# Down projection: seven places instead of three for the raw operands of the block products, and other load and product times in the scheduler

## The chip, the core and the metric

The kernel runs on one core of one Trainium2 chip, as one launch. The metric is the device time of the launch in microseconds (us), the median of several executions; less is better. All data are float32; matmul operands are the 32-bit "fp32r" type, and each product of two float32 operands is made of three matmuls (below).

## What is computed

One inference step of one encoder layer, for 1024 prompt tokens and 32 sample tokens: a normalised input projection, three recurrent mixers (GLA, HGRN2, mLSTM), an output projection, and a feed-forward block with a causal convolution over time. The change lies in the last part, cut here to what matters:

```
def conv_ffn(xn, buf, w_up, conv_w, conv_b, w_down):
    up = xn @ w_up                                   # 1024 -> 2 * 2816
    up, buf = causal_dwconv(up, buf, conv_w, conv_b) # 3 taps
    gate, val = jnp.split(up, 2, axis=-1)
    return (jax.nn.gelu(gate, approximate=True) * val) @ w_down, buf   # 2816 -> 1024
    ...
    x = x + rms_norm(h, g_ffn_post[l])
```

## The kernel before

**Three matmuls per product.** An operand is split into a high half (a cast to fp32r on ScalarE, line 95) and a low half (raw minus high on VectorE, line 98). `mm3` (lines 89 to 91) then adds high x high, high x low and low x high into one PSUM bank. On TensorE every product therefore shows as L89, L90 and L91.

**The stages.** The program runs through the input projection with the mixers and the output projection (tiles `pf`, `pv`, `zp`, `fxt` and the 64-row matmuls of line 773), then the up projection (`pux`, `puw`, `puy`, `puz`; 22 blocks `f` of 128 features, each with its convolution and gelu), then the down projection in `down_all`. The down projection has two parts.

1. The **first part** (tiles `pd`, called the pd stage here) takes 288 token columns (units 0, 8 and 4) the plain way: for each of the 22 `f` it loads `hr` (three pieces of `h_d`, line 1360) and 512 KB of weights `wd` (line 1363), splits both, and does 8 x 3 matmuls of 128x288. Beside that it forms sums of weight blocks (`sums`, lines 1231 to 1234) from pairs of `wd` tiles and stores them to `t_d` (line 1236). `hr` has two buffers, `wd` four (tag `wide`).
2. The **second part** (called the seven products here) takes the other six units of 128 tokens by a Strassen-Winograd scheme of seven block products p1 to p7, run in the order p1, p2, p6, p5, p3, p7, p4. Each is `seven(p, ps, first)`: for `k` = 0 to 10 it loads one raw tile `r` (named `rp` in the profile) in two transfers, 256 KB of weights or weight sums (line 1409) and 192 KB of activations or activation sums (line 1408). From `r` come four halves: `wdp` (weights, high and low in one tile, seven buffers) and `hhp`, `hlp` (activations, two buffers each for odd and for even `k`). Three token units x 3 matmuls of 128x512 follow, into the banks `pdx` (p1, p6, p7, p4), `pdy` (p2) or `pdw` (p5, p3). Between products the banks are copied out or added to `cu` and `cl`; `finish_half` and `finish_end` (lines 1324, 1326, 211, 212, 1335) normalise and add the residual, and line 1336 stores the result.

**Where raw tiles lie.** In before, `r` has tag `y0` with three buffers of the pool `ph` (the pool of the up projection's tiles, which is still open). A fourth load can be issued only when all four halves of the first of the three have been made: when the second subtraction of that tile (`hlp` or `wdp`, line 98) is through. The same pool holds the tags `y1` (one buffer), `bw` (two) and `st` (one), which the up projection fills and nothing uses later.

**What sets the order.** Nothing runs in the order in which it is written. `order` builds a graph of all instructions and `play` places them engine by engine, on its own table of costs; the engine then runs its list in that order, whatever is ready. In that table a load or store issued on SP (SyncE) queues behind the one before, takes its transfer time, and counts as landed 650 ns after that (`stop = queue + 650`); `PRODUCT` gives the time of a matmul by its width. Every cast, subtraction and matmul that depends on a load is placed by these figures, in the whole program. If a load comes later than its place in the list, the engine stands there, and what follows in its list waits too.

Of the kernel before, what the change touches and what calls it, by code (L numbers as in the profile page):

```python
# [9 lines left out]
F32 = mybir.dt.float32  # L10
# [21 lines left out]
NCOL = 2 * HW  # L32
# [9 lines left out]
def fcol(u):  # L42

    return 128 * u if u < 4 else SMP if u == 8 else GAP_P + 2 + 128 * (u - 4)
# [35 lines left out]
def body(ctx: ExitStack, tc: tile.TileContext, a: dict):  # L80
# [1073 lines left out]
    def weight_halves(name, src):  # L1154
        t = praw[1].tile([128, 2, 512], F32R, tag="op", name=name, bufs=7)
        split(t[:, 0], t[:, 1], src, dve)
        return t[:, 0], t[:, 1]
# [71 lines left out]
    def sums(k, ws):  # L1229
        (b11, b12), (b21, b22) = ((t[:, :512], t[:, 512:]) for t in ws)  # L1230
        dve.tensor_tensor(b11, b12, b11, op=ALU.subtract)
        dve.tensor_tensor(b12, b22, b12, op=ALU.subtract)
        dve.tensor_tensor(b22, b22, b11, op=ALU.subtract)
        dve.tensor_tensor(b21, b21, b22, op=ALU.subtract)
        for i in range(2):
            sp.dma_start(t_d[k, i], ws[i])
# [68 lines left out]
    def down_all(ph, p6, gp):  # L1305
        xres = {}

        def wide(name):
            return p6.tile([128, 1024], F32, tag="wide", name=name, bufs=4)

        def residual(u):
            n = 128 if u < 8 else DEC
            x = p6.tile([128, 1024], F32, tag="xres", name=f"fr{u}", bufs=3)
            sp.dma_start(x[:n], x2_d[128 * u:128 * u + n, :])
            xres[u] = x
# [27 lines left out]
        def h_halves(name, w, r, pool_, tag):  # L1343
            hh, hl = (pool_.tile([128, 384], F32R, tag=f"{tag}{x}", name=f"h{x}{name}", bufs=2) for x in "hl")
            split(hh[:, :w], hl[:, :w], r, dve)
            return hh, hl


        off, w = {}, 0
        for u in FIRST:  # L1350
            off[u] = w
# [2 lines left out]
        banks = [p.tile([128, 512], F32, tag=t, name=f"pd0_{i}", bufs=b) for i, (p, t, b) in enumerate(where)]  # L1354
        pair = []
        for f in range(NF):
            r = ph.tile([128, 288], F32, tag="hr", name=f"hr{f}", bufs=2)
            for u in FIRST:
                n = 128 if u < 8 else DEC
                sp.dma_start(r[:, off[u]:off[u] + n], h_d[f, :, fcol(u):fcol(u) + n])  # L1360
            hh, hl = h_halves(f"0_{f}", w, r, ph, "h")
            wr = praw[0].tile([128, 1024], F32, tag="raw", name=f"wd0_{f}r", bufs=2) if f < 2 else                 wide(f"wd0_{f}r")
            sp.dma_start(wr, a["w_dn"][f])
            wd = [weight_halves(f"wd0_{f}{hf}", wr[:, 512 * hf:512 * hf + 512]) for hf in range(2)]
            pair.append(wr)
            if f % 2:
                if f // 2 >= len(EARLY):
                    sums(f // 2, pair)
                pair = []
            if f == NF - 6:  # L1370
                sp.dma_start(gp, a["grows"][1:2, :].broadcast_to([128, 1024]))
                for u in FIRST:
                    residual(u)
            for d in range(8):
                c = slice(128 * (d % 4), 128 * (d % 4) + 128)
                mm3(banks[d][:, :w], [t[:, c] for t in wd[d // 4]], (hh[:, :w], hl[:, :w]), f == 0, f == NF - 1)
# [27 lines left out]
        def seven(p, ps, first):  # L1404
            ops = []
            for k in range(NP):
                r = ph.tile([128, NCOL], F32, tag="y0", name=f"r{p}_{k}", bufs=3)
                sp.dma_start(r[:, :384], ASRC[p](k))
                sp.dma_start(r[:, 384:896], BSRC[p](k))
                hh, hl = h_halves(f"{p}_{k}", 384, r[:, :384], *((ph, "h") if k % 2 else (p6, "g")))  # L1410
                wd = weight_halves(f"wd{p}_{k}", r[:, 384:896])
                ops.append((k, hh, hl, wd))
                if k == NP - 2:
                    continue
                for i in range(3):
                    c = slice(128 * i, 128 * i + 128)
                    for (j, hh, hl, wd) in ops:
                        mm3(ps[i], (hh[:, c], hl[:, c]), wd, first and j == 0, j == NP - 1, skip_group_check=True)
                ops = []
                if k % 3 == 0 and todo:  # L1420
                    todo.pop(0)()
# [173 lines left out]
AHEAD = {"mx": 10000., "psm": 10000., "pdx0": 1400., "pdx1": 700., "pdw0": 1400., "pdw1": 700., "pt": 130000.}  # L1595
ENGINES = ("PE", "DVE", "Activation", "Pool", "SP")
WINDOW = 3413.3
PRODUCT = {512: 232., 384: 175.5, 288: 133.5, 282: 131.5, 274: 126.5, 256: 118.}
PACKET = ((4, 9), (32, 9), (128, 13), (256, 18), (512, 27), (1024, 46), (1536, 65), (2048, 84), (4096, 159), (8192, 330), (1 << 16, 2640))
TABLES = {"Ln": 5, "Gelu_apprx_tanh": 11, "Exp": 0, "Tanh": 0, "Square": 0}  # L1600

# [94 lines left out]
def _product(i):  # L1696
# [9 lines left out]
    if mode == (128, 128) or (mode == (128, 32) and not f32) or mode == (32, 128):  # L1706
        g = PRODUCT.get(n, n / 2.4 + 12) if not f32 else max(n * 2 / 2.4 + 2.5, 60) if tr else 2 * max(n * 2 / 2.4 + 8, 112)
        return g, True, (128, 128) if mode == (128, 32) else mode, cells, (r, sums)
# [160 lines left out]
def play(g, tail, change, slack=None):  # L1869
# [6 lines left out]
    rows, held, seen, known, count = {}, [], [-1] * len(g.pred), dict.fromkeys(ENGINES, -1), 0  # L1876
    port, queue = {"DVE": 0., "Pool": 0.}, 0.
# [24 lines left out]
    while True:  # L1902
        t, e = min(((free[e] if ready[e] else max(free[e], at[wait[e][0][2]]), k) for k, e in enumerate(ENGINES) if ready[e] or wait[e]),
                   default=(None, None))
        if e is None:
            break
        e = ENGINES[e]
        while wait[e] and wait[e][0][0] <= t + 1e-6:
            heapq.heappush(ready[e], heapq.heappop(wait[e])[1:])
        if not ready[e]:  # L1910
            heapq.heappush(ready[e], heapq.heappop(wait[e])[1:])
        if e == "PE" and len(ready[e]) > 1:
            c = min(heapq.nsmallest(12, ready[e]), key=lambda x: x[0] + (change if mm[x[1]][2] != mode else 0))
            ready[e].remove(c)
            heapq.heapify(ready[e])
        else:
            c = heapq.heappop(ready[e])
        n = c[1]
        t = max(t, at[n])
        d, own, lock = cost[n]  # L1920
        sync = max([known[e]] + [seen[q] for q in g.pred[n] if eng[q] != "PE" or e != "PE"])
        if e == "PE" and any(k in rows and rows[k][0] != mm[n][4][0] and rows[k][1] > sync for k in mm[n][4][1]):
            held.append(c)
            continue
        if e == "SP" and queue - t - 1400 > BACKLOG:
            heapq.heappush(ready[e], c)
            free[e] = queue - 1400 - BACKLOG + 5
            continue
        if e == "Pool" and lock and port["DVE"] > t:
            heapq.heappush(ready[e], c)  # L1930
            free[e] = port["DVE"] + 5
            continue
        if e == "SP":
            free[e] = t + own
            queue = max(t + 1400, queue) + d
            stop = queue + 650
        elif e == "PE":
            d, wide, m, cl, (row, sums) = mm[n]
            if mode not in (None, m):
                t = max(t, max(cells) + (93 if mode == (128, 128) else 45))  # L1940
            mode, t = m, max([t] + [cells[c] for c in cl])
            if wide:
                free[e] = clock.run(t, d)
                cells = [free[e]] * 16
                stop = free[e] + 166
            else:
                f = clock.factor(t)
                for c in cl:
                    cells[c] = t + d * f
                clock.add(t, 14)  # L1950
                free[e] = t + 14 * f
                stop = t + d * f + 168
        else:
            if e == "DVE" and lock:
                t = max(t, port["Pool"])
                port["DVE"] = t + d
            if e == "Pool" and lock == 1:
                port["Pool"] = t + d
            if g.table[n] not in (None, table):
                table = g.table[n]  # L1960
                t += 1283
            free[e], stop = t + own, t + d
        if e == "PE":
            rows.update((k, (row, count)) for k in sums)
            seen[n], count = count, count + 1
            if sync > known[e]:
                while held:
                    heapq.heappush(ready[e], held.pop())
        else:
            seen[n] = sync  # L1970
        known[e] = sync
        start[n], end[n] = t, stop
        seq[e].append(n)
        release(n)
# [143 lines left out]
```

## Time and profile before

| | |
|---|---|
| median of 3 runs | 1357.84 us (1354.48 to 1359.75) |
| the profiled execution | 1356.24 us |
| its span in the trace | 1354.4 us |
| TensorE (PE) busy | 1303.9 us, 96% of the span |
| VectorE (DVE) busy | 1039.2 us, 77% |
| ScalarE (ACT) busy | 710.6 us, 52% |
| GpSimd (POOL) busy | 181.9 us, 13% |
| moved by DMA | 285.24 MB, mean 211 GB/s |

The profiled execution lies 1.84 us above its span (what lies outside the first and last instruction) and 1.6 us below the median. PE busy is the union of modelled, pipelined matmuls: a lone matmul is shown with 0.39 us while back to back ones start more closely, so that a short wait of PE can vanish in it. In the profile, "idle before, releaser" after a group says how long its engine stood idle just before it and what ended that. SPq rows are transfers being issued on SP's queue; "DMA rp<-t_d" is the flight of such a transfer until it landed.

### The profile page before, as it was taken

To read this page: it belongs to the slowest core of one execution; us is meant where nothing else is said; L and a number is where in the kernel's file an instruction comes from. 1 tells how busy PE (TensorE), PEld (TensorE's weight loads), DVE (VectorE), ACT (ScalarE), POOL (GpSimd) and SP (SyncE) were. 2 spreads that over 40 slices of the span, in tenths; PEclk is the share of its full clock that TensorE was granted. 3 is DMA by queue.
4 is the path that set the end of the run, shared out by engine and by line. 5 is a ranking of instruction groups with operands and counts; after the bars stand their busy time and mean duration, and the time that the engine had idled before them with its cause. 6 is when DMAs were issued, how large, how long until landed. Compare 5 with 4: busy or idle time off the path is not lost.

```text
span 1354.4 us, 30370 instructions
## 1 busy us (share of the span) xinstructions
PE 1303.9 (96%) x11977; PEld 1207.9 (89%) x11977; DVE 1039.2 (77%) x1884; ACT 710.6 (52%) x1400; POOL 181.9 (13%) x331
## 2 busy tenths in 40 slices
PE   6999999999999999999899999999999999998997
PEld 5999999998898887678899999999999999886775
DVE  6795549757889468878899988888888877755576
ACT  5654556545576554436754544545545454555554
POOL 2010100100102112222012211111111110000011
PEclk9999999999999999999999999999999999999998
DMA  9899869976898964635156623323223189786675
GB/s 327 260 330 332 266 243 333 301 260 203 287 305 288 331 231 121 202 95 171 69 199 230 215 97 109 102 87 119 80 87 119 71 275 290 261 265 192 218 248 205
DMA packets 148422, 285.24 MB, mean 211 GB/s; under 512 B 30039, under 2 KB 84471, under 8 KB 148279
## 3 DMA queue, kind: packets, MB, share of 16 engines
q1 hardware_dynamic: 148279, 283.30, 62.2%
q8 instruction: 94, 1.54, 0.5%
q14 instruction: 49, 0.40, 0.1%
HBM read 201.90 MB, written 81.34 MB: 209 GB/s over the span
## 4 chain that ended last, share of the span: by engine, by line
PE 69%; DMA 14%; DVE 9%; ACT 4%; issue 3%; SPq 1%; POOL 0%; DVEq 0%; ACTq 0%; POOLq 0%
PE pux L91 4%; PE pux L89 4%; PE pux L90 4%; PE pv L89 4%; PE pv L91 4%; PE pv L90 4%; DMA rp<-t_d 4%; PE pf L89 3%; PE pf L91 3%; PE pf L90 3%; PE puw L90 3%; PE puw L91 3%; PE puw L89 3%; DMA rp<-in_w_dn 2%; PE zp L89 2%
## 5 line engine op out<-in xcount | busy, mean ns | idle before, releaser
L1250 DVE SCALAR_TENSOR_TENSOR y<-uu,fconv_sb,y 128x1060 f32<-128x1060 f32 x88 | 115.8, 1320 | 7.9 <-ACT y L1248 7.4
L98 DVE TENSOR_TENSOR wdp<-rp,wdp 128x512 fp32r<-128x512 f32 x77 | 53.2, 691 | 56.2 <-ACT wdp L95 55.9
L95 ACT CAST wdp<-rp 128x512 fp32r<-128x512 f32 x77 | 47.7, 620 | 70.4 <-DMA rp<-t_d 39.0
L1248 ACT ACTIVATE y<-uu,fconv_sb 128x1060 f32<-128x1060 f32 x44 | 56.1, 1278 | 25.9 <-POOL uu L1245 21.5
L1196 ACT COPY c<-pux 128x274 f32<-128x274 f32 (+1 forms) x132 | 46.3, 381 | 33.9 <-PE pux L91 30.1
L926 POOL TENSOR_TENSOR hrs<-hss,mhalf 128x5 f32<-128x5 f32 (+3 forms) x27 | 35.8, 1330 | 175.3 <-DVE hss L925 172.6
L89 PE MATMUL pv<-wt_0h,xh 128*128 128x256 f32 (+2 forms) x195 | 53.8, 297 | 2.6 <-DVE xl L309 1.3
L91 PE MATMUL pv<-wt_0h,xl 128*128 128x256 f32 (+2 forms) x195 | 51.7, 288 | 0.0
L90 PE MATMUL pv<-wt_0l,xh 128*128 128x256 f32 (+2 forms) x195 | 51.5, 287 | 0.0
L89 PE MATMUL pdx<-wdp,hhp 128*128 128x512 f32 x132 | 44.8, 404 | 6.7 <-ACT hhp L95 4.6
L89 PE MATMUL pv<-wt_1h,xh 128*128 128x256 f32 (+2 forms) x195 | 49.1, 288 | 0.0
L91 PE MATMUL pv<-wt_1h,xl 128*128 128x256 f32 (+2 forms) x195 | 48.6, 288 | 0.0
L1245 POOL COPY uu<-fcache_sb 128x2 f32<-128x2 f32 x44 | 23.4, 531 | 186.1 <-DVE uu L1201 186.1
L90 PE MATMUL pv<-wt_1l,xh 128*128 128x256 f32 (+2 forms) x195 | 48.3, 288 | 0.0
L98 DVE TENSOR_TENSOR hlp<-rp,hhp 128x384 fp32r<-128x384 f32 x77 | 41.8, 552 | 5.4 <-ACT hhp L95 2.9
L90 PE MATMUL pdx<-wdp,hhp 128*128 128x512 f32 x132 | 43.9, 395 | 0.0
L91 PE MATMUL pdx<-wdp,hlp 128*128 128x512 f32 x132 | 42.9, 395 | 0.1
L95 ACT CAST hhp<-rp 128x384 fp32r<-128x384 f32 x77 | 38.4, 511 | 5.8 <-PE pdx L90 3.1
L89 PEld LDWEIGHTS pv<-wt_0h,xh 128*128 128x128 f32 (+1 forms) x195 | 35.2, 189 | 4.6 <-DVE xl L309 1.6
L211 POOL TENSOR_SCALAR gss<-gss 128x1 f32<-128x1 f32 (+1 forms) x9 | 7.4, 817 | 233.7 <-ACT gjk L1324 158.2
L89 PEld LDWEIGHTS pdx<-wdp,hhp 128*128 128x128 f32 x132 | 24.8, 191 | 13.9 <-ACT hhp L95 6.7
L808 DVE COPY_PREDICATED P<-masks_sb,sc 128x352 f32<-128x352 int32 (+1 forms) x44 | 29.8, 678 | 8.8 <-PE sc L773 8.3
(1781 smaller groups left out, 5144.4 us busy)
## 6 DMA issues: line engine op xcount, KB each, us to landing
h_d<-y SPq DMA_DIRECT2D x22, 530.0 KB, 5.1
rp<-t_d SPq DMA_DIRECT2D x44, 256.0 KB, 3.8
wt_0r<-in_w_tok SPq DMA_DIRECT2D x21, 512.0 KB, 5.9
wt_1r<-in_w_tok SPq DMA_DIRECT2D x21, 512.0 KB, 5.0
rp<-in_w_dn SPq DMA_DIRECT2D x33, 256.0 KB, 3.7
rp<-s_d SPq DMA_DIRECT2D x44, 192.0 KB, 3.9
wt_0l<-lt_d SPq DMA_DIRECT2D x14, 512.0 KB, 4.7
wt_1l<-lt_d SPq DMA_DIRECT2D x14, 512.0 KB, 5.8
```

Source lines behind the costliest of these rows:

```text
L89: pe.matmul(ps, lh[0], rh[0], start=first, stop=False, **kw)
L90: pe.matmul(ps, lh[0], rh[1], start=False, stop=False, **kw)
L91: return pe.matmul(ps, lh[1], rh[0], start=False, stop=last, **kw)
L95: act.copy(hi, src)
L98: (eng or pool).tensor_tensor(lo, src, hi.bitcast(F32), op=ALU.subtract)
L211: pool.tensor_scalar(out, ss, other, EPS, op0=ALU.add, op1=ALU.add)
L808: dve.copy_predicated(dst, mk_.broadcast_to([n, 11, *mk_.shape[2:]]), src)
L926: pool.tensor_tensor(rs[:n, h0:h0 + nh], ss[:n, h0:h0 + nh], mhalf[:n, :nh], op=ALU.pow)
L1196: act.copy(t, ps)
L1245: pool.tensor_copy(u[:, GAP_S:GAP_S + 2], fcache[:, j, :])
L1248: act.activation(y, u, AF.Identity, scale=fconv[:, j, 2:3], bias=fconv[:, j, 3:4])
L1250: dve.scalar_tensor_tensor(y, uu[i][:, s:s + NCOL], fconv[:, j, s:s + 1], y, op0=ALU.mult, op1=ALU.add)
```

## The change

- The raw tiles of the seven products go round seven places: `y0`, `bw`, `y0`, `y1`, `y0`, `bw`, `st`. All seven are 128x896 or larger already, so no memory is added. The fourth load no longer waits for the first tile, the eighth does.
- In the pd stage, `hr` uses the two `bw` buffers for every other pair of `f`, which makes four places of two.
- In the cost table a transfer counts as landed 1250 ns after its transfer time instead of 650 ns, and the six matmul times move by 0.5 to 4.5 ns.

```
+        places = [("y0", 3), ("bw", 2), ("y0", 3), ("y1", 1), ("y0", 3), ("bw", 2), ("st", 1)]
+        def raw(name):
+            t, b = places[count[0] % 7]
+            count[0] += 1
+            return ph.tile([128, 896], F32, tag=t, name=name, bufs=b)
...
-            r = ph.tile([128, 288], F32, tag="hr", name=f"hr{f}", bufs=2)
+            r = ph.tile([128, 288], F32, tag="hr", name=f"hr{f}", bufs=2) if f % 4 < 2 else \
+                ph.tile([128, 288], F32, tag="bw", name=f"hr{f}", bufs=2)
...
-                r = ph.tile([128, NCOL], F32, tag="y0", name=f"r{p}_{k}", bufs=3)
+                r = raw(f"r{p}_{k}")
...
-PRODUCT = {512: 232., 384: 175.5, 288: 133.5, 282: 131.5, 274: 126.5, 256: 118.}
+PRODUCT = {512: 227.5, 384: 175., 288: 132.5, 282: 131., 274: 127., 256: 119.5}
...
-            stop = queue + 650
+            stop = queue + 1250
```

Since the cost table serves the whole program, the lists of all engines change from the first stage on, with the same work in them. Two places matter for the prediction.

ScalarE, at the start of p6 (raw tiles `rp_k` with the weight halves `wdp_k` and the activation halves `hhp_k`; the last number only names a buffer). Before:

```order
L95 CAST wdp_2_15961<-rp_2_15954 128x512
L95 CAST wdp_3_15980<-rp_3_15973 128x512
L95 CAST hhp_2_15957<-rp_2_15954 128x384
L95 CAST hhp_3_15976<-rp_3_15973 128x384
L1324 ACTIVATE gjk_16560,gss_16559<-cu_15693 128x512
L95 CAST wdp_4_15999<-rp_4_15992 128x512
L95 CAST hhp_4_15995<-rp_4_15992 128x384
```

The same place of the changed kernel:

```order
L95 CAST wdp_3_15980<-rp_3_15973 128x512
L95 CAST hhp_0_15919<-rp_0_15916 128x384
L95 CAST wdp_4_15999<-rp_4_15992 128x512
L95 CAST hhp_3_15976<-rp_3_15973 128x384
L95 CAST wdp_5_16018<-rp_5_16011 128x512
L95 CAST hhp_2_15957<-rp_2_15954 128x384
L95 CAST hhp_4_15995<-rp_4_15992 128x384
```

Before, the activation cast of tile 2 stands behind the weight cast of tile 3, the newest of the tiles on its way; the two casts of a tile are neighbours. In the changed kernel the weight casts run up to three tiles ahead of the activation casts.

SP, in the last third of the pd stage (`hr` and `wd` are that stage's loads, `t_d<-wd` its stores, `rp_k` the first loads of p1). Before:

```order
L1363 DMA wd_15r<-in_w_dn 128x1024
L1409 DMA rp_2_15476<-in_w_dn 128x512
L1360 DMA hr_14964<-h_d 128x128 x2
L1360 DMA hr_14964<-h_d 128x32
L1408 DMA rp_2_15476<-h_d 128x384
L1236 DMA t_d<-wd_12r 128x1024
L1360 DMA hr_15004<-h_d 128x128 x2
L1360 DMA hr_15004<-h_d 128x32
L1236 DMA t_d<-wd_13r 128x1024
```

The same place of the changed kernel:

```order
L1372 DMA wd_15r<-in_w_dn 128x1024
L1417 DMA rp_2_15476<-h_d 128x384
L1418 DMA rp_4_15537<-in_w_dn 128x512
L1369 DMA hr_15050<-h_d 128x128 x2
L1369 DMA hr_15050<-h_d 128x32
L1417 DMA rp_4_15537<-h_d 128x384
L1236 DMA t_d<-wd_12r 128x1024
L1369 DMA hr_15090<-h_d 128x128 x2
L1369 DMA hr_15090<-h_d 128x32
L1418 DMA rp_6_15575<-in_w_dn 128x512
L1417 DMA rp_6_15575<-h_d 128x384
L1236 DMA t_d<-wd_13r 128x1024
```

Ahead of the last `wd` load (`wd_21r`) before has issued three raw tiles of p1 (0, 1 and 2), the changed kernel six (0, 3, 2, 4, 6 and 1); three more tiles of 448 KB have moved from the seven products into the pd stage.

More of the change, by code (lines that the diff above doesn't have):

```diff
@@ L1346, in h_halves @@
             return hh, hl
+        places = [("y0", 3), ("bw", 2), ("y0", 3), ("y1", 1), ("y0", 3), ("bw", 2), ("st", 1)]
+        count = [0]
+        def raw(name):
+            t, b = places[count[0] % 7]
+            count[0] += 1
+            return ph.tile([128, 896], F32, tag=t, name=name, bufs=b)
         off, w = {}, 0
```

## Prediction

> **What bounds the kernel now.** First the page's table of engines: TensorE (PE) is busy nearly throughout, so a gain must come from stretches in which it waits or is clocked down. The stages one by one show where; columns are stretch, length, then busy time with number of instructions for PE, PEld, DVE, ACT, POOL, then granted clock, DMA share and GB/s.
>
> ```profile
> 0.00:620.00 620.00, 594.37 (x6960) 537.28 (x6961) 449.70 (x982) 330.45 (x688) 82.12 (x126) 0.99 0.78 260
> 620.00:1098.50 478.50, 473.06 (x3774) 468.55 (x3773) 414.84 (x607) 247.13 (x447) 84.31 (x182) 1.00 0.36 127
> 1098.50:1171.70 73.20, 70.94 (x528) 69.56 (x527) 59.73 (x101) 38.81 (x74) 2.10 (x5) 1.00 0.92 302
> 1171.70:1197.30 25.60, 25.60 (x128) 21.06 (x127) 19.25 (x35) 14.76 (x35) 4.60 (x6) 1.00 0.79 252
> 1197.30:1221.00 23.70, 23.17 (x101) 18.23 (x99) 12.39 (x22) 12.93 (x25) 0.00 (x0) 1.00 0.74 234
> 1221.00:1245.40 24.40, 21.83 (x92) 17.13 (x93) 15.50 (x28) 12.20 (x24) 0.00 (x0) 1.00 0.62 199
> 1245.40:1295.40 50.00, 47.53 (x207) 38.37 (x206) 25.89 (x45) 25.92 (x50) 0.00 (x0) 1.00 0.66 211
> 1295.40:1346.80 51.40, 47.42 (x199) 37.70 (x197) 37.97 (x65) 27.70 (x60) 6.62 (x9) 0.97 0.70 232
> 1346.80:1354.40 7.60, 0.00 (x0) 0.00 (x0) 3.91 (x6) 0.69 (x2) 2.12 (x4) 0.74 0.55 208
> ```
>
> The rows are: mixers and projections, up projection, pd stage, then p1, p2, p6, p5 with p3, p7 with p4, and the tail. The up projection leaves PE 5.4 us idle in 478. The seven products leave more than their busy column says, because a lone matmul is shown longer than its turn. The turn is read where nothing is waited for, from the starts of two groups of three:
>
> ```profile
> 1201.36 0.84 PE L89 MATMUL pdy<-wdp,hhp 128*128 128x512 f32 x3
> ...
> 1202.04 0.84 PE L90 MATMUL pdy<-wdp,hhp 128*128 128x512 f32 x3
> ...
> 1173.75 0.44 PE ptxw L1389 x4
> ```
>
> 0.68 us for three is 0.227 us each. The products hold 7 x 11 x 9 = 693 such matmuls, 157.1 us, and 24 transposes in six groups of four at 0.44 us (last row, from the chain of waits), 2.6 us. With a few last `pd` matmuls that is 160 us, in a stage of 175.1 us (1171.7 to 1346.8): **15 us of slack**, mostly from p6 on. What ends it, in the waits:
>
> ```profile
> ACT wdp L95 <- DMA rp<-t_d: 39.0, 33, 2.1
> ACT wdp L95 <- DMA rp<-in_w_dn: 28.6, 22, 2.9
> ...
> PE pdx L89 <- ACT hhp L95: 4.6, 4, 2.0
> PE pdx L89 <- DVE cl L1454: 2.1, 1, 2.1
> PE pdw L89 <- ACT hhp L95: 1.7, 1, 1.7
> ...
> PE pdw L89 <- ACT cl L1445: 0.8, 1, 0.8
> ...
> PE pdy L89 <- ACT hhp L95: 0.2, 1, 0.2
> ```
>
> ScalarE stands 67.6 us before loads and passes some on to PE as missing `hhp`. One turn of one place shows how (p6, tile 2, then tile 5 in the same place):
>
> ```profile
> 1219.07 0.32 SPq L1409 DMA_DIRECT2D rp<-t_d  x1
> ...
> 1222.22 0.62 ACT L95 CAST wdp<-rp 128x512 fp32r<-128x512 f32 x1 [1.29 <-DMA rp<-t_d]
> ...
> 1224.64 0.62 ACT L95 CAST wdp<-rp 128x512 fp32r<-128x512 f32 x1 [1.80 <-DMA rp<-t_d]
> 1225.17 0.92 ACT L95 CAST hhp<-rp 128x384 fp32r<-128x384 f32 x2
> ...
> 1225.73 0.97 PE L89 MATMUL pdx<-wdp,hhp 128*128 128x512 f32 x3 [2.02 <-ACT hhp L95]
> 1225.90 1.02 DVE L98 TENSOR_TENSOR hlp<-rp,hhp 128x384 fp32r<-128x384 f32 x2
> ...
> 1226.48 0.32 SPq L1409 DMA_DIRECT2D rp<-t_d  x1
> ```
>
> Issue 1219.07, cast 3.15 us later; then ScalarE, whose list has the weight cast of tile 3 next, waits until 1224.64, and tile 2's activations, long there, are cast at 1225.17. Only the subtraction behind that frees the place: 7.41 us for three tiles, where PE needs 3 x 9 x 0.227 = 6.13. So two things bind: three places, and a list made for loads landing earlier than they do.
>
> **The change, part by part.** *(a) Seven places.* With PE at full pace a place comes round every 7 x 2.04 = 14.3 us. It is held from issue to landing and for its casts (all instructions on `rp`: least, median and longest ns):
>
> ```profile
> L95 ACT CAST hhp<-rp x77: 494/511/526, 1110.3 to 1341.1; 128x384 fp32r<-128x384 f32 x77
> L98 DVE TENSOR_TENSOR hlp<-rp,hhp x77: 535/552/559, 1114.6 to 1341.8; 128x384 fp32r<-128x384 f32 x77
> L95 ACT CAST wdp<-rp x77: 605/621/625, 1165.1 to 1337.7; 128x512 fp32r<-128x512 f32 x77
> L98 DVE TENSOR_TENSOR wdp<-rp,wdp x77: 673/692/694, 1165.8 to 1338.3; 128x512 fp32r<-128x512 f32 x77
> L1409 SPq DMA_DIRECT2D rp<-t_d x44: 319/320/663, 1213.2 to 1334.5; - x44
> L1408 SPq DMA_DIRECT2D rp<-s_d x44: 422/432/1464, 1213.7 to 1310.0; - x44
> ...
> DMA to landing us min/median/max: 2.9/4.0/5.6
> ```
>
> Taking the slowest landing, 5.6, plus the 4.3 us from first cast (1222.22) to the end of both subtractions (1226.48) in the bad turn above, it is 9.9 us, 4.4 us to spare. Bandwidth allows it: 448 KB per 2.04 us is 225 GB/s, which p2 (234) already moved. SP issues two transfers per tile, 0.75 us of 2.04; the four halves cost ScalarE 1.13 and VectorE 1.24 us of 2.04. Result stores stand in SP's list among these loads, and SP stands at each until VectorE has its `fr`; what queues behind has those 4.4 us in hand. So PE becomes the bound. What is late next are the bank turns: the 0.8 us before p3 (`cl` copies) stays; of the 2.1 before p4 about 1.2 stays (the add into `cl` takes 0.68 and has other VectorE work ahead of it). With 1.5 for the start of p1 and for ScalarE's turn order, 3.5 us remain. Gain: 15 - 3.5 = **11.5 us**. Ends: the five PE rows above sum to 9.4 us, and if only these go, less the 3.5, it is 6; and 14 if only 1 us stays.
>
> *(b) The pd stage.* Four `hr` places remove ScalarE's waits for `hr` and so at most PE's 2.2 us. Against that, three raw tiles of 448 KB each now share this stage's transfers, which already move 302 GB/s at a DMA share of 0.92:
>
> ```profile
> ACT hh L95 <- DMA hr<-h_d: 9.0, 8, 2.7
> ...
> PE pd L89 <- ACT hh L95: 2.2, 5, 0.7
> ...
> 1139.91 5.46 DMA wd_17r<-in_w_dn
> ```
>
> 1.38 MB at 302 GB/s is 4.6 us, and a `wd` flight of 5.5 us is on the chain that ends last here. In SP's list the added loads stand ahead of `wd_16r` to `wd_21r`, so these, their sums and their stores queue behind. Ends: -2.2 and +4.6; the middle, **+1 us**, since neither row outweighs the other.
>
> *(c) Landing at 1250 ns and matmul times.* In the seven products this is in (a): activation casts no longer stand behind the newest load. Elsewhere the lists change with the same work. The trace has no row for that; the nearest is PE's idle time, 25.6 us in the first 620 and 5.4 in the up projection. I take **0**, with ends of 7 us either way: about a quarter of those 31 us.
>
> *The tail* after the last matmul (7.6 us) has the same instructions: 0.
>
> **Sum**: -11.5 + 1 + 0 = -10.5 us, 1345.7 for the profiled execution's 1356.24. That execution lies 1.6 below the median, so for the median 1357.84 - 10.5 = **1347.3 us**, 0.8% faster. What a measurement here can tell from no change is about 0.5%, 6.8 us.
>
> **Rivals.** *Crowded pd stage.* All 4.6 us of (b) are lost and (a) gives its low 6: 1357.84 - 6 + 4.6 = 1356.4. For it speaks the share of 0.92; against, that the same bytes leave the products, where there is room.
>
> *Loads were never the bound.* If a turn took the least landing (2.9 us), 0.75 for its two issues and 1.7 for its chain of halves (0.62, 0.51 and 0.55), it would be 5.35, under 6.13, and three places would do; only the two bank turns would shift. Then perhaps 2 us go: 1356. Against it: the measured turn of 7.41 and the median landing of 4.0. The Trainium skill ("DMA: Bandwidth & Descriptors", Anatomy of one DMA — SWDGE (gpsimd) path) has a rule that would say this: about 2.0 us fixed plus bytes at 436 GB/s, so by estimate 2.6 us for 256 KB, stated for the GpSimd path. The trace disagrees for SP's loads: 4.0 us.
>
> *Slower: the first 620 us lose their clock.* A gap of about 2 us halves TensorE's pace after it, as before p4:
>
> ```profile
> 1321.36 0.68 DVE L1454 TENSOR_TENSOR cl<-cl,pdx 128x512 f32<-128x512 f32 x1
> ...
> 1322.18 0.47 PE L89 MATMUL pdx<-wdp,hhp 128*128 128x512 f32 x1 [2.12 <-DVE cl L1454]
> ...
> 1323.62 0.63 PE L90 MATMUL pdx<-wdp,hhp 128*128 128x512 f32 x1
> ...
> 1324.05 0.63 PE L89 MATMUL pdx<-wdp,hhp 128*128 128x512 f32 x1
> ```
>
> The starts are 0.43 apart instead of 0.227; the granted clock of 0.97 over these 51.4 us is a loss of 1.5 us, so 2.1 + 1.5 = 3.6 us per gap. The new lists of the mixer stage, where PE hangs on casts and 64-row work, could hold more such gaps. From five more on (18 us) the forecast's gain is turned into a loss of more than the bound: 1347.3 + 18 = 1365.3. For it: every list there changes; against: with 600 ns more the table's landing is nearer to what the loads take, so waits should get fewer. (The Trainium skill, "TensorE: Matmul & The Clock Gate", Part 1, names an idle window of about 3.4 us for the halving; here 2.1 us of idle sufficed.)
>
> *The early stages gain too*, by (c)'s full 7 us: 1340.3.
>
> **How the numbers follow.** Forecast 0.62, crowded 0.11, never the bound 0.08, slower 0.08, early gain 0.11. Range: from the early gain with (a) at its 14, 1357.84 - 14 + 1 - 7 = 1338, to the two rivals at 1356 with 2 us of spread, 1358; what lies outside is the slower case and an edge of the others. Faster by over 0.5% (below 1351): 0.60 of the forecast's 0.62, and the early gain: 0.71. Within 0.5%: both middle rivals and the forecast's 0.02: 0.21. Slower: 0.08.
>
> **What would show it.** Right: in the seven products PE's rows add to some 163 to 165 us; ScalarE's waits for `rp` fall from 67.6 to under 20; `PE <- ACT hhp` all but goes; the granted clock of p7 and p4 is 1.00. The pd stage shows its cost as longer waits of `wd` casts for loads. Wrong: the products still take over 170 us, or the stretch up to the first `pd` matmul differs from 1098.5 by over 7 us.

## The result and the profile after

The changed kernel takes 1348.71 us, the median of five executions (1344.93 to 1350.66), against 1357.84 for before (1352.63 to 1360.38): a ratio of 0.994, 95% interval 0.9911 to 0.9969, or 9.1 us less where 10.5 were forecast. Its profiled execution is the fastest of the five: 1344.93 us, span 1343.1, against 1356.24 and 1354.4.

Before's span, cut at three places that both kernels have: the first matmul of the up projection (`pux`), the first of p2 (`pdy`), the end of the last matmul. Columns are those of the stages in the prediction.

```profile
0.00:633.90 633.90, 608.26 (x7021) 548.67 (x7022) 461.91 (x992) 342.43 (x709) 85.27 (x128) 0.99 0.77 258
633.90:1197.30 563.40, 555.70 (x4365) 547.77 (x4364) 481.61 (x732) 288.71 (x532) 87.86 (x191) 1.00 0.45 155
1197.30:1346.70 149.40, 139.92 (x595) 111.43 (x593) 91.64 (x157) 78.74 (x159) 6.52 (x9) 0.99 0.68 220
1346.70:1354.40 7.70, 0.03 (x1) 0.00 (x0) 4.01 (x7) 0.69 (x2) 2.23 (x4) 0.74 0.54 205
```

The changed kernel at the same places:

```profile
0.00:636.90 636.90, 609.41 (x7020) 547.48 (x7021) 461.59 (x992) 343.14 (x709) 88.44 (x128) 0.99 0.77 257
636.90:1198.90 562.00, 554.60 (x4361) 546.70 (x4361) 479.73 (x732) 290.77 (x536) 88.44 (x191) 1.00 0.46 157
1198.90:1335.40 136.50, 136.00 (x599) 111.97 (x597) 93.06 (x155) 78.70 (x155) 7.28 (x11) 1.00 0.72 234
1335.40:1343.10 7.70, 0.00 (x0) 0.00 (x0) 4.11 (x7) 0.69 (x2) 1.50 (x3) 0.80 0.54 205
```

| stretch | before | after | difference |
|---|---|---|---|
| start to first `pux` (mixers, projections) | 633.9 | 636.9 | +3.0 |
| first `pux` to first `pdy` (up projection, pd stage, p1) | 563.4 | 562.0 | -1.4 |
| first `pdy` to the last `pdx` (p2 to p4) | 149.4 | 136.5 | -12.9 |
| tail | 7.7 | 7.7 | 0 |

PE's pause in p2 to p4 falls from 9.5 us (149.40 - 139.92) to 0.5, and its clock there rises from 0.99 to 1.00. The waits of the changed kernel in p2 to p4 show who waits for whom now:

```profile
ACT hhp L95 <- PE pdx L90: 13.1, 15, 2.2
...
DVE hlp L98 <- PE pdw L91: 10.6, 13, 1.6
...
DVE hlp L98 <- DMA rp<-s_d: 2.2, 3, 0.7
ACT wdp L95 <- DMA rp<-in_w_dn: 2.1, 2, 1.3
...
ACT hhp L95 <- DMA rp<-s_d: 1.5, 2, 0.7
ACT wdp L95 <- DMA rp<-t_d: 1.5, 2, 1.0
```

The casts of weights wait 3.6 us for loads (2.1 + 1.5), against 58.2 in the same stretch of before (its two rows stand under e3 below); ScalarE and VectorE now wait for PE to give up `hhp` and `hlp`. The same can be seen at the turn from p2 to p6, and something that was not forecast:

```profile
1219.00 0.32 SPq L1418 DMA_DIRECT2D rp<-t_d  x1
...
1219.29 0.39 PE L89 MATMUL pdx<-wdp,hhp 128*128 128x512 f32 x1
...
1220.40 0.52 ACT L95 CAST hhp<-rp 128x384 fp32r<-128x384 f32 x1 [1.42 <-PE pdy L90]
...
1223.80 0.52 ACT L95 CAST hhp<-rp 128x384 fp32r<-128x384 f32 x1 [1.64 <-PE pdy L90]
...
1224.50 0.84 PE L91 MATMUL pdy<-wdp,hlp 128*128 128x512 f32 x3
```

p6 (`pdx`) begins at 1219.29 while p2 (`pdy`) goes on until after 1224.50. The list that PE has now laps one product over the next, and so the bank turns have cover.

### The profile page after: what moved, and what is told of

Its sections match the earlier page's. It is cut to its first block, busy times and chain, and to the rows that moved or that the text cites. A ratio compares the mean times of both kernels' runs of the same rounds, so it can differ in the third digit from the quotient of the medians.

```text
span 1343.1 us, 30434 instructions
## 1 busy us (share of the span) xinstructions
PE 1300.0 (97%) x11977; PEld 1206.1 (90%) x11977; DVE 1038.5 (77%) x1884; ACT 713.3 (53%) x1400; POOL 185.7 (14%) x331
## 4 chain that ended last, share of the span: by engine, by line
PE 81%; DMA 7%; DVE 7%; ACT 3%; issue 2%; SPq 0%; POOL 0%; DVEq 0%; ACTq 0%; POOLq 0%
PE pux L89 5%; PE pux L90 5%; PE pux L91 5%; PE pv L89 4%; PE pv L90 4%; PE pv L91 4%; PE pf L89 3%; PE puw L91 3%; PE puw L89 3%; PE puw L90 3%; PE pf L91 3%; PE pf L90 3%; PE zp L89 2%; PE pdx L89 2%; PE pdx L90 2%; PE pdx L91 2%
## 5 line engine op out<-in xcount | busy, mean ns | idle before, releaser
L98 DVE TENSOR_TENSOR hlp<-rp,hhp 128x384 fp32r<-128x384 f32 x77 | 42.6, 556 | 37.6 <-ACT hhp L95 12.2
L926 POOL TENSOR_TENSOR hrs<-hss,mhalf 128x5 f32<-128x5 f32 (+3 forms) x27 | 40.7, 1532 | 172.3 <-DVE hss L925 172.1
L91 PEld LDWEIGHTS pv<-wt_0h,xl 128*128 128x128 f32 (+1 forms) x195 | 34.2, 189 | 0.8 <-issue 0.4
```

The source lines that it names most:

```text
L91: return pe.matmul(ps, lh[1], rh[0], start=False, stop=last, **kw)
L98: (eng or pool).tensor_tensor(lo, src, hi.bitcast(F32), op=ALU.subtract)
L926: pool.tensor_tensor(rs[:n, h0:h0 + nh], ss[:n, h0:h0 + nh], mhalf[:n, :nh], op=ALU.pow)
```

## The experiments

Each kernel is timed beside before on the same chip: e1 to e4 on one chip (before's median there 1353.44 us), a2, e5, e10 and e11 on a second (1354.76), e6, e8, e12 and e13 on a third (1354.57). The ratio to that median has its 95% interval behind it; the other columns come from each kernel's one profile. "Load waits" are ScalarE's and VectorE's waits for `rp` in p2 to p4. "Idle" is the stretch up to the first `pux` less PE's busy time in it. "Clock loss" is the same stretch cut into 31 equal windows, (1 - granted clock) x length summed.

| kernel | ratio | first `pux` | idle | clock loss | `pux` to `pdy` | p2 to p4 | load waits |
|---|---|---|---|---|---|---|---|
| before | 1 | 633.9 | 25.6 | 4.9 | 563.4 | 149.4 | 59.9 |
| after | 0.994 [0.9911, 0.9969] | 636.9 | 27.5 | 5.1 | 562.0 | 136.5 | 7.8 |
| a2_after | 0.9955 [0.9935, 0.9974] | 637.8 | 24.1 | 10.5 | 566.2 | 136.3 | 9.5 |
| e1_places | 0.9902 [0.9877, 0.9927] | 628.9 | 22.4 | 3.2 | 563.1 | 136.8 | 16.2 |
| e2_costs | 0.9962 [0.9945, 0.998] | 637.4 | 26.4 | 6.8 | 563.3 | 141.3 | 53.3 |
| e3_late_rp | 0.994 [0.9917, 0.9963] | 634.1 | 24.7 | 6.5 | 561.7 | 140.3 | 54.3 |
| e4_places_late_rp | 0.9897 [0.9873, 0.9922] | 634.8 | 25.3 | 6.8 | 563.1 | 136.3 | 15.3 |
| e8_four | 0.9865 [0.9826, 0.9904] | 629.4 | 24.3 | 3.5 | 560.3 | 136.2 | 35.2 |
| e5_hr_two | 0.9966 [0.9944, 0.9988] | 636.0 | 26.6 | 6.8 | 565.9 | 136.2 | 7.9 |
| e6_p1_three | 0.9879 [0.9842, 0.9917] | 630.2 | 24.2 | 3.3 | 561.3 | 136.4 | 12.1 |
| e10_old_product | 0.9895 [0.9865, 0.9925] | 631.9 | 24.0 | 5.1 | 563.9 | 136.1 | 10.7 |
| e11_old_landing | 0.9956 [0.9935, 0.9977] | 636.9 | 24.9 | 8.4 | 564.6 | 136.4 | 12.0 |
| e12_half | 0.9865 [0.9833, 0.9897] | 628.1 | 23.2 | 3.2 | 561.7 | 136.0 | 10.1 |
| e13_mirror | 0.9843 [0.981, 0.9875] | 621.2 | 21.0 | 0.0 | 565.3 | 137.3 | 12.2 |

Eleven of the fourteen kernels share three sets of lists up to the first `pux`: the order of instructions on every engine is the same in the traces of before, e1, e3 and e4, in those of after, a2, e2 and e5, and in those of e6, e8 and e10 (but for up to 35 places in 7020 of PE's, all 64-row matmuls whose recorded starts change places). The first `pux` spans 628.9 to 634.8 in the first set, 636.0 to 637.8 in the second and 629.4 to 631.9 in the third. So one list gives up to 5.9 us of spread between profiles, and a single profile can't tell two lists apart by less.

The theory was that the ring of three places bound the products (R in the expectations); the first rival, that it was the order of the lists, made for loads landing too early (O).

### What freed the products

**e1_places**: the places alone, with the old cost table.

```
-                r = ph.tile([128, NCOL], F32, tag="y0", name=f"r{p}_{k}", bufs=3)
+                r = raw(f"r{p}_{k}")
```

(with `raw`, its table of seven and the four places of `hr`)

> Seven places and the four hr places, with the cost table of before (landing 650 ns, old matmul times). The lists of all engines up to the middle of the up projection are those of before. Theory R (the ring of three places binds): p2 to p4, from the first pdy matmul to the end of the last pdx matmul, falls from 149.5 us to 136 to 140; pd stage with p1 is 99 to 101 us against 98.8; the time is 8 to 12 us under before. Rival O (the list made for early landing binds, places matter little): p2 to p4 stays above 144 us and the time is within 5 us of before.

p2 to p4 take 136.8 us: the places alone take away 12.6 of the 12.9. The time is 13.4 us under before (1353.44 - 1340.08), more than R's 8 to 12. The kernel as a whole looks better than with the whole change (0.9902; the whole change 0.994 and, repeated, 0.9955); its interval is clear of that of the repeat, not of that of the first measurement.

**e2_costs**: the cost table alone, three places.

```
-PRODUCT = {512: 232., 384: 175.5, 288: 133.5, 282: 131.5, 274: 126.5, 256: 118.}
+PRODUCT = {512: 227.5, 384: 175., 288: 132.5, 282: 131., 274: 127., 256: 119.5}
...
-            stop = queue + 650
+            stop = queue + 1250
```

> Three places as before, with the cost table of the changed kernel (landing 1250 ns, new matmul times) for the whole program; the mixers and projections have the lists of the changed kernel. Theory R: p2 to p4 stays between 145 and 150 us, since a place still takes over 7 us for three tiles; the time is 0 to 4 us under before. Rival O: p2 to p4 falls below 143 us. Rival H (the new lists of the early stages give the gain): the first pd matmul comes over 4 us earlier than in before, and the time is 6 us or more under before with p2 to p4 unchanged.

**e3_late_rp**: before, with 1250 ns for the loads into `rp` alone.

```
+        self.late.append(name.startswith("rp"))
...
-            stop = queue + 650
+            stop = queue + (1250 if g.late[n] else 650)
```

> Before, with the landing of 1250 ns for the raw tiles of the seven products alone (three places, all else 650 ns). The lists up to the end of the pd stage are those of before but for a few rows. Theory R: p2 to p4 146 to 150 us, the time within 4 us of before. Rival O: p2 to p4 below 143 us, the time 6 us or more under before.

Here R missed. With three places p2 to p4 still come down to 141.3 and 140.3 us, by 8 to 9. The waits of e3 in p2 to p4 show that this isn't mainly because loads are waited for less:

```profile
ACT wdp L95 <- DMA rp<-t_d: 36.6, 32, 2.6
ACT wdp L95 <- DMA rp<-in_w_dn: 15.9, 12, 2.8
...
PE pdx L89 <- ACT hhp L95: 1.3, 2, 1.1
```

Before, in the same stretch, the first two were:

```profile
ACT wdp L95 <- DMA rp<-t_d: 39.0, 33, 2.1
ACT wdp L95 <- DMA rp<-in_w_dn: 19.2, 15, 2.8
```

ScalarE waits 52.5 us instead of 58.2, yet PE waits 1.3 for these `hhp` where it waited 4.6. ScalarE's list at that place of e3 tells why:

```profile
1224.33 0.62 ACT L95 CAST wdp<-rp 128x512 fp32r<-128x512 f32 x1 [1.30 <-DMA rp<-t_d]
1225.13 0.52 ACT L95 CAST hhp<-rp 128x384 fp32r<-128x384 f32 x1 [0.17 <-DMA rp<-s_d]
1226.69 0.62 ACT L95 CAST wdp<-rp 128x512 fp32r<-128x512 f32 x1 [1.05 <-DMA rp<-t_d]
1227.27 0.51 ACT L95 CAST hhp<-rp 128x384 fp32r<-128x384 f32 x1
```

Here each tile's activations follow its own weights. In before's list the activations of tile 2 stood behind the wait for tile 3, and went out late by that much.

**e4_places_late_rp**: both of these remedies, matmul times as before.

```
 (the edit of e1_places and that of e3_late_rp)
```

> Seven places and four hr places, 1250 ns for the raw tiles of the seven products alone, the rest of the cost table as in before: the lists of the mixers and projections are those of before. Theory R: p2 to p4 135 to 138 us and the time 9 to 12 us under before, at most 2 us better than seven places alone. Rival O: over 4 us better than seven places alone. Rival H: since the early lists are those of before, over 4 us worse than the changed kernel.

136.3 us. So the two remedies are for the same waits: 12.6 by places, 9.1 by the order (149.4 - 140.3), 13.1 by both. The time is 13.1 us under before, above R's 9 to 12; it is no better than with places alone (0.9897 and 0.9902), and H, which had it 4 us worse than the changed kernel, falls.

**e8_four**: four places, all transfers at 1250 ns, old matmul times.

```
-        places = [("y0", 3), ("bw", 2), ("y0", 3), ("y1", 1), ("y0", 3), ("bw", 2), ("st", 1)]
+        places = [("y0", 3), ("y0", 3), ("y0", 3), ("y1", 1)]
```

> Four places (three y0 and y1) for the raw tiles, with hr on bw, landing 1250 ns and the old matmul times; the lists up to the pd stage are those of the changed kernel with the old matmul times. A place then turns in 8.2 us of PE time for four tiles, against landing plus casts of some 6.5 us. Theory R+ (a ring of three is short by under one tile once the list is right): p2 to p4 within 1.5 us of the 136 us of seven places. Rival: it falls halfway, 138 to 140 us, because the slow landings of over 5 us need more places.

136.2 us: with lists made for 1250 ns, one place more than three is enough. Four places with the old table were not run. In its p2 to p4 ScalarE still waits 34.8 us for loads, and PE keeps going:

```profile
DVE wdp L98 <- ACT wdp L95: 30.2, 31, 2.3
ACT wdp L95 <- DMA rp<-t_d: 25.4, 23, 2.5
...
ACT wdp L95 <- DMA rp<-in_w_dn: 9.4, 9, 1.9
```

One of its six executions took 3197.4 us; it is left out of the ratio, and its cause is unknown.

### The pd stage

**e5_hr_two**: the changed kernel with `hr` on two buffers again.

```
-            r = ph.tile([128, 288], F32, tag="hr", name=f"hr{f}", bufs=2) if f % 4 < 2 else \
-                ph.tile([128, 288], F32, tag="bw", name=f"hr{f}", bufs=2)
+            r = ph.tile([128, 288], F32, tag="hr", name=f"hr{f}", bufs=2)
```

> The changed kernel with hr on its two buffers alone, so that bw belongs to the raw tiles from the first. My term for the pd stage said at most 2.2 us for the four hr places: the time is 0 to 2.5 us over the changed kernel, and the stretch from the first pux to the first pdy matmul 0 to 2.5 us longer. Rival: the hr places cost by holding back tile 1 of p1, which then lands too late; then it is 0 to 3 us under.

**e6_p1_three**: three places for p1, so that p1's early loads can't crowd the pd stage, seven from p2 on; old matmul times.

```
-            t, b = places[count[0] % 7]
+            t, b = places[count[0] % 7] if count[0] > 10 else ("y0", 3)
```

> Seven places from p2 on, but three for p1, with landing 1250 ns and the old matmul times: the first loads of p1 no longer move into the pd stage beyond before's three. If the crowding of the pd stage costs (my term: 4.6 us at most), the stretch from the first pux to the first pdy matmul is 1 to 4 us shorter than with seven places throughout (563.9), and the time 0.986 to 0.989 of before. If not, p1 itself misses its places: the stretch is 0 to 2 us longer and the time 0.989 to 0.992.

By their times both are inconclusive. e5 (0.9966) lies in the interval of its yardstick a2_after (0.9955), e6 (0.9879) in that of e10_old_product (0.9895), though e6's time and its stretch of 561.3 both fall where the crowding was to put them. From the first `pux` to the first `pdy` the changed kernel itself took 562.0 and 566.2 us in its two profiles; differences of 1 or 2 us can't be told within that. What can be told is where the waits went. In the changed kernel, from the first `pd` to the first `pdy`:

```profile
ACT wd L95 <- DMA wd_16r<-in_w_dn: 3.9, 1, 3.9
ACT wd L95 <- DMA wd_21r<-in_w_dn: 3.7, 1, 3.7
ACT wd L95 <- DMA wd_20r<-in_w_dn: 2.9, 1, 2.9
...
PE pd L89 <- ACT hh L95: 1.9, 2, 1.4
...
ACT wd L95 <- DMA hr<-h_d: 1.0, 1, 1.0
```

ScalarE's waits for `wd_16r` to `wd_21r` rose from 10.2 us to 17.2 and those for `hr` fell from 9.0 to 1.0; PE's wait for `hh` went from 2.2 to 1.9.

All fourteen profiles together tell more. Take PE's idle time from the first `pd` to the first `pdy` and add the clock loss there (in windows of 5 us). In the five kernels that give p1 fewer than seven places it is 2.3 (before), 0.9 (e2), 1.9 (e3), 0.8 (e8) and 1.5 us (e6). In the nine that give it seven it is 2.0 (e12), 2.4 (after), 4.2 (e4), 4.6 (e13), 4.7 (e10), 4.8 (e11), 5.2 (e1), 6.0 (a2) and 6.2 (e5). In seven of these nine, and in none of the five, 1.7 us of it is lowered clock. The means are 1.5 and 4.5: seven places in p1 go with some 3 us more lost in this stage. With one profile per kernel this is a strong tendency, not a proof. (e1 took 102.6 us from the first `pd` to the first `pdy`, where 99 to 101 were expected.) The changed kernel's own profile, at 2.4, is one of the luckiest of its group.

### The early stages

**a2_after**: the changed kernel again, as the yardstick for e5, e10 and e11.

> The changed kernel once more, as the yardstick for this group, since seven places alone came out at 0.990 of before and the changed kernel at 0.994. Theory H- (the new lists of the early stages cost some 5 us): 0.993 to 0.996 again. Rival N (the difference was the draw of clock gaps and the chip): 0.989 to 0.992.

**e10_old_product**: the changed kernel with the old matmul times.

```
-PRODUCT = {512: 227.5, 384: 175., 288: 132.5, 282: 131., 274: 127., 256: 119.5}
+PRODUCT = {512: 232., 384: 175.5, 288: 133.5, 282: 131.5, 274: 126.5, 256: 118.}
```

> The changed kernel with the old matmul times; the landing stays at 1250 ns for every transfer. Theory H- with the landing as its cause: as the changed kernel, 0.993 to 0.996, the first pux matmul at 636 us or later in the profile. H- with the matmul times as its cause: 0.989 to 0.991, pux from 632 to 635. p2 to p4 136 to 138 us by either.

**e11_old_landing**: the changed kernel with 650 ns.

```
-            stop = queue + 1250
+            stop = queue + 650
```

> The changed kernel with the old landing of 650 ns; the new matmul times stay. H- with the landing as its cause: 0.989 to 0.991. H- with the matmul times as its cause: 0.993 to 0.996. p2 to p4 136 to 138 us by either, since seven places forgive the early lists.

The matmul times cost 0.6% (0.9955 and 0.9956 with the new ones, 0.9895 with the old ones), 5.7 and 7.6 us by the medians (1346.24 and 1348.17 against 1340.59). Much of it lies ahead of the first `pux`: 636.0 to 637.8 in the five profiles with the new times (after, a2, e2, e5 and e11), 628.9 to 634.8 in the seven with the old ones. The landing time elsewhere than in `rp` has no cost that can be told: e10 (0.9895) and e4 (0.9897) differ in that alone.

Two theories were then open: that new times push back the first score matmuls (S: `sc` starts at 197.2 in the changed kernel, at 155.7 in e10), or that each list of the early stages simply draws its own time (L).

**e12_half**: matmul times halfway between old and new. **e13_mirror**: moved as far to the other side.

```
e12:
+PRODUCT = {512: 229.75, 384: 175.25, 288: 133., 282: 131.25, 274: 126.75, 256: 118.75}
e13:
+PRODUCT = {512: 236.5, 384: 176., 288: 134.5, 282: 132., 274: 126., 256: 116.5}
```

> The changed kernel with matmul times halfway between the old and the new. The first score matmul (sc, line 773) stands at row 1032 of PE's list, against 948 with the old times and 1162 with the new. Theory S (the mixers start later in the list and so end later): the first sc at 165 to 185 us, the first pux between 632 and 637, the time 0.990 to 0.994 of before. Rival L (a lottery: every new list of the early stages draws a new time): pux anywhere from 629 to 638, unrelated to sc.

> The changed kernel with the matmul times moved the other way by the same amounts (old minus the change), so further from what the trace shows. The first score matmul stands at row 948 as with the old times, though some 1500 rows of PE's list differ. Theory S: first sc near 156 us, first pux 629 to 635, 0.988 to 0.992 of before. Rival T (times further from the truth cost time): 0.996 or more. Rival L: anywhere from 0.988 to 0.997.

Both are well clear of the changed kernel (0.9865 and 0.9843). Against e10, with the old times, their intervals overlap, and e8, which has e10's early lists, reaches 0.9865 too. The score matmuls (least, median and longest ns, first and last start) of e13:

```profile
L773 PE MATMUL sc<-Qz,Ld x1344: 178/219/268, 155.5 to 570.4; 64*64 64x32 f32 x116, 64*64 64x64 f32 x67, 64*32 64x16 f32 x6, 64*32 64x32 f32 x3
```

and of e10:

```profile
L773 PE MATMUL sc<-Qz,Ld x1344: 179/219/366, 155.7 to 580.4; 64*64 64x32 f32 x115, 64*64 64x64 f32 x68, 64*32 64x16 f32 x8, 64*32 64x32 f32 x1
```

S falls: `sc` starts at the same time in both, but ends 10 us apart, and the first `pux` is at 621.2 and 631.9. In e12 the first `sc` is at 172.0, as S had it, but the first `pux` at 628.1 and not at 632 or later. T falls with e13's 0.9843. L is what is left, but it missed as well: it had `pux` at 629 or later in e12 and 0.988 or more in e13. It isn't shown, either, that the draw is blind. In order of the 512-column time that the table counts (227.5, 229.75, 232, 236.5), the first `pux` is at 636.0 to 637.8, 628.1, 628.9 to 634.8 and 621.2, so that longer counted times might by themselves make better lists. e12 lies within 0.8 us of the spread of the old lists; only e13 and the changed kernel's lists stand apart. More tables would be needed to tell.

The table says what differs. First `pux`, less idle, less clock loss, leaves 600.2 to 604.3 us in all fourteen profiles (e13 600.2, e10 602.8, after 604.3), while the first `pux` itself spans 621.2 to 637.8. So the profiles differ in how long PE pauses there, and in how much clock it loses, and part of that differs from one execution to the next of the same list.

For the changed kernel one such place can be named. Rows of its trace, on SP, VectorE and PE:

```profile
497.13 0.33 SPq L692 DMA_DIRECT2D gt<-g_d  x1
...
501.10 0.48 DVE L924 TENSOR_TENSOR cat<-hn,gt 32x320 f32<-32x320 f32 x1 [5.50 <-DMA gt<-g_d]
...
502.10 0.52 DVE L808 COPY_PREDICATED P<-masks_sb,sc 32x176 f32<-32x176 int32 x1
502.72 0.53 DVE L808 COPY_PREDICATED P<-masks_sb,mi 32x352 f32<-32x352 int32 x1
...
503.31 0.99 PE L773 MATMUL og<-v,P 32*32 32x64 f32 x11 [3.34 <-DVE P L808]
```

VectorE comes to the product with the gate `gt` at 495.6, 1.5 us before that load is even issued, and stands 5.50 us. Behind it in its list are the copies into `P`, and for `P` PE waits 3.34 us. In e10 the load is issued at 494.81 and the product stands 8 us further on:

```profile
494.81 0.33 SPq L692 DMA_DIRECT2D gt<-g_d  x1
...
504.00 0.47 DVE L924 TENSOR_TENSOR cat<-hn,gt 32x320 f32<-32x320 f32 x1
```

What follows in PE's clock (last but two in a row), the changed kernel first, then its repeat, then e10:

```profile
496.00:502.00 6.00, 3.86 (x52) 2.92 (x50) 0.80 (x2) 3.31 (x8) 1.50 (x3) 1.00 0.97 319
502.00:508.00 6.00, 4.70 (x22) 3.82 (x23) 5.58 (x9) 1.61 (x4) 0.70 (x1) 0.72 0.41 161
```

```profile
496.00:502.00 6.00, 4.51 (x54) 3.45 (x52) 1.64 (x4) 3.31 (x8) 1.71 (x3) 1.00 0.87 275
502.00:508.00 6.00, 5.64 (x22) 4.60 (x23) 5.03 (x8) 2.56 (x6) 1.56 (x2) 0.53 0.70 271
```

```profile
496.00:502.00 6.00, 6.00 (x75) 5.08 (x74) 4.40 (x10) 3.31 (x8) 0.87 (x2) 1.00 0.88 294
502.00:508.00 6.00, 6.00 (x28) 4.89 (x28) 5.40 (x12) 4.09 (x10) 1.95 (x3) 1.00 0.95 314
```

The pause of 3.34 us and 0.28 x 6 = 1.7 us of clock make 5.0 us; in the repeat 1.75 and 0.47 x 6 = 2.8 make 4.6. e2 and e5, with the same early lists, have the same stand (6.2 and 5.3 us for `gt`); no kernel with other matmul times shows a wait of VectorE for `gt`. In e11, with the new times but 650 ns, VectorE stands 2.8 us for `gt` and PE only 0.3 us here; its larger clock loss (8.4) comes from other places, so this one stand doesn't explain all five kernels. Nor do the totals show all of its price. Of the 5.0 us between the first `pux` of the changed kernel and of e10, 3.5 are idle time, and the pause of 3.34 accounts for nearly all of that; the clock loss is 5.1 in both, since e10 loses its clock elsewhere. In the repeat the idle time is that of e10 (24.1 and 24.0) and the clock loss 5.4 larger. So the price of this stand is read from the trace around it and not shown by a run; a kernel with that one load moved ahead was not tried.

e13 has the lowest median and ratio of all (0.9843), its interval clear of those of before and of the changed kernel, but not of those of e6, e8 and e12. Its matmul times are further from what the trace shows (227 ns for 512 columns, counted as 236.5). Its gain lies in the early stages, with the least idle time and no lowered clock before the up projection; whether that is luck stays open.

## Why the prediction was right

**(a) Seven places, -11.5: right, a little small; which part of the change earns it was not seen.** p2 to p4 gave 12.9 us. The 3.5 us that were to remain in the seven products were the mis-sized part: the six from p2 on hold 594 matmuls, 134.8 us at 0.227, and they take 136.5, so 1.7 remain. The bank turns that were to stay (0.8 before p3, 1.2 before p4) went, as the new list laps one product over the next. "So two things bind: three places, and a list made for loads landing earlier than they do" was right as mechanism, but the gain was put down to the places as a whole. Each of the two alone removes most (e1 12.6, e3 9.1), and with lists made for 1250 ns a fourth place is enough. From the first `pdx` to the end (1172.7 to 1335.4) the products take 162.7 us, beside the 163 to 165 named; a few more `pd` matmuls now lie within that.

**(b) The pd stage, +1: the right sign, but too small.** The waits moved as described, `hr` to `wd`. In the profile that was forecast nothing came of it: PE's own pause from the first `pux` to the first `pdy` went from 7.7 us (563.40 - 555.70) to 7.4, and the stretch by -1.4, less than the 4 us between two profiles of the same kernel. As far as the other profiles show, that was luck: with seven places in p1 PE loses some 3 us more here (2.0 to 6.2 against 0.8 to 2.3). The weak step was to weigh the two rows alike. The saving by `hr` places is there where p1 has few places (PE waits 0.2 us for `hh` in e6 and 0.8 in e8, against 2.2 before); with seven the longer `wd` waits outweigh it (1.9 in the changed kernel, 2.7 in its repeat).

**(c) Lists elsewhere, 0: this is the step that failed.** The early stages lost 3.0 us in the profile. Over four profiles each, the first `pux` lies at 632.9 us on average with before's early lists and at 637.0 with the changed kernel's, 4.1 later, and the two sets don't overlap. "Elsewhere the lists change with the same work" was taken as no reason for a sign; the ends of 7 us held. What was drawn is more pauses and lowered clock; why the new matmul times draw it stays open. It hid in the sum because (a) gave 1.4 more and the middle stretch 1.4 less: +3.0 - 1.4 - 12.9 = -11.3 for the span, -10.5 forecast. The median shows 9.1; the profiled execution of the changed kernel happened to be its fastest. So the mechanism of (a) was right, and that the sum came within 1.4 us is partly luck: a gain larger than forecast against losses that were put at nothing or too small.

**The rivals.** *Loads were never the bound* falls with e1 and e3. *Crowded pd stage* had the right waits and, at some 3 us of its 4.6, most of its price; its low 6 for (a) was wrong. *The first 620 us lose their clock* named a mechanism that is there: one more pause of 1.8 to 3.3 us with a lowered clock behind it, 4.6 to 5.0 us where it stands, one place where five were feared, and each at 1 to 1.5 us more than the 3.6 taken. *Early stages gain too* was no outcome of this list, but of e13 it would have been (12.7 us less up to the first `pux`).

## What to carry to other kernels

Don't price a wait by its sum: 60 us of waits for loads cost PE 9.4 us in one list, and 54 us cost it 2.0 in another, and what decides is which cast stands behind the waiting one in an engine that runs in order. A ring that is just short can be mended by more places, and in large part by telling the scheduler when loads really land (12.6 and 9.1 us here); with the second, one more place was enough. Try each alone before taking both, and look at what the extra places let in early: seven of them crowded the stage before. When an edit of a cost table draws every list anew, time it apart from the rest of the change, look first at pauses of PE over 1.5 us in stages that the edit wasn't meant for, and try several tables, since the truest need not draw the best list. Profile one list more than once before calling a few us of a stage its own: here the same list differed by up to 5.9.

## What had not been expected of the hardware

A pause of 1.75 us was followed by a granted clock of 0.53 over the next 6 us (a2_after, the windows above):

```profile
502.36 1.48 PE L773 MATMUL og<-v,P 32*32 32x64 f32 x12 [1.75 <-DVE P L808]
```

The Trainium skill ("TensorE: Matmul & The Clock Gate", Part 1) names an idle window of about 3.4 us for this; the measurement here is the shorter one. Not each such pause is answered. In e13 PE pauses 2.2 us (`pb` for `vf`, near 452) and in e6 2.55 us (`pv` for `xl`, before 166.7), and neither loses any clock. Of the pauses between matmuls ahead of the first `pux` in the fourteen profiles, all eleven of 2.6 us or more (2.63 to 4.07) were followed by a granted clock of 0.50 to 0.76 over the next 6 us, the shorter ones only in part. That goes with the spread between executions of one program: the five of the changed kernel have spans of 1343.1 us at a mean granted clock of 0.995, 1343.7 at 0.993, 1346.8 at 0.992, and 1347.1 and 1348.9 at 0.990.
